# Half as many rows per DMA engine in an ifftshift of an 8192 x 8192 float32 matrix

## The chip, the core and the metric

The kernel runs on one core of one Trainium2 chip. The number that counts is the device time of one execution in microseconds; several runs are taken and their median is given. The profile is of one further execution with the hardware profiler on.

## The reference

```python
def setup_inputs():
    return {"x": np.random.randn(8192, 8192).astype(np.float32)}

def reference(x: np.ndarray) -> np.ndarray:
    return np.fft.ifftshift(x)
```

For even sizes an ifftshift over both axes swaps the four quadrants: `out[r, c] = x[(r + 4096) % 8192, (c + 4096) % 8192]`. Nothing is calculated. 268.4 MB are read from the device's memory and 268.4 MB are written to it.

## The kernel before

All the work is done by DMAs that go from the input tensor straight to the output tensor; no tile in on-chip memory is used and no compute engine has work. A row of the matrix has 8192 floats, 32 KB; a half row has `hc` = 4096 floats, 16 KB. `hr` = 4096 is half the number of rows.

The helper `both` (lines 25 to 34; the DMA itself has line 27 in the profile) issues one DMA on a queue. Its access pattern has three levels, `[[C, rows], [hc, 2], [1, piece]]` on the output: `rows` consecutive rows, in each row both halves, and in each half one contiguous run of `piece` floats that begins at column `col`. On the input side the same rows stand `hr` rows further on (modulo `R`), and the halves are taken in the opposite order (the step of the second level is `-hc`), so that each half lands in the other one.

The loops in lines 40 to 42 go over blocks of rows, and inside a block over the two values of `col`, 0 and `piece`. With `piece = hc // 2` (2048 floats, 8 KB) a DMA moves one quarter of both halves; the second DMA of a block moves the other quarter of the same rows. All DMAs are issued from SyncE (SP), on one queue, in the order of the loops.

A DMA is spread over the core's 16 DMA engines along its outermost level: with `rows = ENGINES * apart` (line 39) each engine gets `apart` neighbouring rows, so neighbouring engines work `apart` rows from each other. With `apart = 4` a DMA covers 64 rows, and each engine moves 4 rows x 2 halves = 8 packets of 8 KB. A further packet of 4 bytes on each engine then adds one to the DMA's semaphore; when all 16 have done so, the DMA has landed.

The framework gives the DMAs eight semaphores in turn (numbers 99 to 106 in the trace). SP issues the ninth DMA when the first has landed, the tenth when the second has, and so on: eight DMAs are in flight. These waits are not written in the kernel. Line 57 (start of the program) and line 68 (end of it) are what the profile gives for the launch code.

Of the kernel before, what the change touches and what calls it, by code (L numbers as in the profile page):

```python
# [1 line left out]

# [4 lines left out]


ENGINES = 16  # L10


@with_exitstack
def kernel(
    ctx: ExitStack,
    tc: tile.TileContext,
    x: bass.AP,
    out: bass.AP,
):
    nc = tc.nc  # L20
    R, C = x.shape
    hr = R // 2
    hc = C // 2

    def both(queue, row, col, rows, piece):

        queue.dma_start(
            out=bass.AP(out.tensor, out.offset + row * C + col, [[C, rows], [hc, 2], [1, piece]]),
            in_=bass.AP(
                x.tensor,  # L30
                x.offset + (row + hr) % R * C + hc + col,
                [[C, rows], [-hc, 2], [1, piece]],
            ),
        )


    apart = 4
    piece = hc // 2
    rows = ENGINES * apart
    for row in range(0, R, rows):  # L40
        for col in (0, piece):
            both(nc.sync, row, col, rows, piece)


# [1 line left out]
_INS = ['x']  # L46
_OUTS = [((8192, 8192), 'float32')]


def kernel(**inputs):  # L50
    import numpy as _np
    import concourse.bacc as _bacc
    import concourse.tile as _tile
    from concourse import mybir as _mybir
    from concourse.bass_utils import run_bass_kernel_spmd as _run

    nc = _bacc.Bacc("TRN2", target_bir_lowering=False, num_devices=1)  # L57
    arrays, args = {}, []
    for name in _INS:
        a = _np.ascontiguousarray(inputs[name])  # L60
        if a.dtype.kind in "iu":
            a = a.astype(_np.int64)
        arrays[f"in_{name}_dram"] = a
        args.append(nc.dram_tensor(f"in_{name}_dram", a.shape, _mybir.dt.from_np(a.dtype), kind="ExternalInput").ap())
    for i, (shape, dtype) in enumerate(_OUTS):
        dt = _mybir.dt.from_np(_np.dtype(dtype))
        args.append(nc.dram_tensor(f"out_{i}_dram", shape, dt, kind="ExternalOutput").ap())
    with _tile.TileContext(nc) as tc:
        kernel(tc, *args)
    r = _run(nc, [arrays], core_ids=[0])  # L70
    got = tuple(r.results[0][f"out_{i}_dram"] for i in range(len(_OUTS)))
    return got[0]
```

## Time and profile before

| | |
|---|---|
| median of 3 runs | 811.06 us (810.79 to 811.39) |
| the profiled execution | 810.44 us |
| its span, first to last instruction | 808.7 us |
| DMAs on SP's queue | 256 of 1024 KB, 25.1 us median from issue to landing |
| packets on that queue | 36864: 32768 of 8 KB and 4096 of 4 bytes |
| read / written in the device's memory | 268.44 MB / 268.44 MB, together 664 GB/s over the span |

How to read it: with no compute, the span is a chain of DMA traffic. The DMA row of the page gives, for 40 equal slices, the mean busy share of the 16 DMA engines in tenths (9 is 90% or more), and the GB/s row below it what they moved (bytes counted once, though each is read and written). Section 3 of the page gives the packets of each queue, and the share of 16 engines' span in which packets were running. An engine counts as busy while a packet of its own is under way, whether the packet moves at full speed or is held up. SP is shown by its waits.

### The profile page before, as it was taken

Reading aid. Unit: us, or ns where it says so; the run is one execution under the profiler, and the core shown is the slowest. Engines: PE = TensorE matmul, PEld = TensorE weight load, DVE = VectorE, ACT = ScalarE, POOL = GpSimd, SP = SyncE. Lnnn points to the kernel's source line nnn. Section 1 sums busy time; section 2 is a strip of 40 time slices with the busy share of each in tenths; the row PEclk is TensorE's granted clock in tenths of the full one; section 3 lists DMA queues with packets and bytes.
Section 4 is the critical chain, followed back from the end, with each engine's and each line's share of the span. In section 5 each row is a group of like instructions: output and inputs, shape, how many; then the busy total and the mean of one; then the engine's idle time right before and its main releaser. Section 6 shows DMA issues by size and latency. Waiting matters only on the chain. (4 is left out here: it accounts for less than half of the span.)

```text
span 808.7 us, 301 instructions
## 1 busy us (share of the span) xinstructions
POOL 0.2 (0%) x4
## 2 busy tenths in 40 slices
POOL 0000000000000000000000000000000000000000
DMA  8999999999999999999999999999999999999998
GB/s 301 331 335 329 336 334 330 335 332 336 332 335 334 336 331 334 339 328 335 331 335 339 334 334 337 331 336 330 336 334 331 339 332 334 333 336 331 337 335 294
DMA packets 36866, 268.47 MB, mean 332 GB/s; under 512 B 4096, under 2 KB 4096, under 8 KB 4096
## 3 DMA queue, kind: packets, MB, share of 16 engines
q1 hardware_dynamic: 36864, 268.45, 99.3%
q14 instruction: 2, 0.02, 0.0%
HBM read 268.44 MB, written 268.44 MB: 664 GB/s over the span
## 5 line engine op out<-in xcount | busy, mean ns | idle before, releaser
L57 POOL MEMSET const-bfloat16-1.0<- 128x1 bf16 x1 | 0.1, 102 | 0.0
L57 POOL MEMSET const-uint8-127<- 128x1 uint8 x1 | 0.1, 102 | 0.0
L57 POOL MEMSET const-float32-1.0<- 128x1 f32 x1 | 0.1, 99 | 0.0
L57 POOL MEMSET const-float32-0.0<- 128x1 f32 x1 | 0.1, 98 | 0.2 <-issue 0.2
## 6 DMA issues: line engine op xcount, KB each, us to landing
out_dram<-in_x_dram SPq DMA_DIRECT2D x256, 1024.0 KB, 25.1
```

The lines of the kernel that those rows point to most:

```text
L57: nc = _bacc.Bacc("TRN2", target_bir_lowering=False, num_devices=1)
```

## The change

```diff
--- before.py
+++ after.py
@@ -34,7 +34,7 @@
         )
 
 
-    apart = 4
+    apart = 2
     piece = hc // 2
     rows = ENGINES * apart
     for row in range(0, R, rows):
```

`rows` becomes 32. The loop over rows has 256 blocks in place of 128, and there are 512 DMAs of 0.5 MB in place of 256 of 1 MB. Each engine has 2 rows x 2 halves = 4 packets of 8 KB in a DMA, followed by its 4-byte packet. Neighbouring engines work 2 rows (64 KB) from each other in place of 4 rows (128 KB), the 16 engines of a DMA span 1 MB of each tensor in place of 2 MB, and an engine comes to the other quarter of its rows after 4 packets in place of 8. The 8 KB runs, the one queue, the eight semaphores and the bytes moved are the same.

## The prediction

> **What bounds the kernel now.** I read the page first, for who is busy at all:
>
> ```profile
> span 808.7 us, 301 instructions
> POOL 0.2 (0%) x4
> ...
> DMA  8999999999999999999999999999999999999998
> GB/s 301 331 335 329 336 334 330 335 332 336 332 335 334 336 331 334 339 328 335 331 335 339 334 334 337 331 336 330 336 334 331 339 332 334 333 336 331 337 335 294
> DMA packets 36866, 268.47 MB, mean 332 GB/s; under 512 B 4096, under 2 KB 4096, under 8 KB 4096
> ...
> q1 hardware_dynamic: 36864, 268.45, 99.3%
> ```
>
> No engine computes; the 16 DMA engines have a packet under way 99.3% of the span. The rate is flat: the inner slices lie between 328 and 339 GB/s. The 4096 packets under 512 B are the semaphore packets, 16 for each of 256 DMAs. Next, SP's own waits, to see if issuing holds the engines up:
>
> ```profile
> SPq L27 <- DMA out_dram<-in_x_dram: 634.0, 248, 3.2
> SPq L68 <- DMA out_dram<-in_x_dram: 24.1, 4, 15.2
> ```
>
> SP waits 634.0 us in 248 waits, 2.56 us each, for a landing before it may issue the next DMA: it is idle, not late. Then the view of stretches (columns: from:to, length, POOL busy, TensorE clock, DMA share, GB/s):
>
> ```profile
> 2.50:5.00 2.50, 0.00 (x0) 1.00 0.83 334
> 6.00:13.00 7.00, 0.00 (x0) 1.00 1.01 349
> 13.00:50.00 37.00, 0.00 (x0) 1.00 1.00 330
> 50.00:400.00 350.00, 0.00 (x0) 1.00 1.00 333
> 400.00:750.00 350.00, 0.00 (x0) 1.00 1.00 334
> ```
>
> Last, the single packet records of the trace. From 3.4 to 5.0 us nearly every 8 KB packet takes 309 ns, and the rate is 420 GB/s. From 6 to 13 us hardly any does: they take 380 ns on the mean, none under 309 and none over 526, at 349 GB/s. From 20 us on 62% take at most 316 ns and the rest are held up, to 1507 ns at worst; the mean is 391 ns, and 16 x 8192 B / 391 ns = 335 GB/s. So an engine alone could do its 2048 packets in 2048 x 309 ns = 633 us; it needs 2048 x 391 ns = 801 us, because 168 us of it are stalls. They come at nearly the same total rate whether all packets are slowed alike or a few are slowed much. I read that as a limit which the 16 engines share, on the memory's side (664 GB/s read and written), and not a limit of an engine or of SP.
>
> **The parts of the change.** The span splits into 2.2 us to the first packet, 805.4 us to the end of the last, and 1.1 us of ending. The profiled execution (810.44) is 0.6 us below the median; I add differences to the median, 811.06.
>
> *Twice the DMAs on SP.* 256 more issues of 562 ns (the records of line 27) are 144 us of SP's queue. A DMA of half the size takes 805.4 / 512 = 1.57 us of the engines, so SP issues for 0.56 us and still waits about 1.0 us each time: 0 on the path. If the cover were gone, 512 x 0.6 us = 307 us would still be below 805. At the start the first eight issues follow each other by 0.65 to 0.73 us, and a half DMA at the unhindered rate lasts 4 x 309 ns = 1.24 us: also covered.
>
> *Half the bytes in flight.* Eight DMAs are in flight as before. When one has landed, seven are left, 7 x 1.57 = 11.0 us of work in place of 22. The first and the last engine to finish a DMA are 1.9 us apart on the mean and 3.0 at most (landings on its semaphore), so the fastest engine still has about 8 us; from an issue to its first packet pass 1.45 us (0.73 to 2.18). Cost 0. The landing time should fall from 25.1 to about 8 x 1.57 = 12.6 us.
>
> *256 more semaphore packets on each engine.* Such a packet is recorded with 9 ns; the next data packet starts 3 ns after the end of the last one in place of 3 ns before it, so it costs 6 ns: 256 x 6 ns = 1.5 us. Ends: 0, where the stalls of the shared limit swallow it, and 256 x 9 ns = 2.3 us. I take 1.5, as 62% of the packets run at the engine's own pace. The packets behind a semaphore show no further cost. I followed each engine's packets from one semaphore to the next (2668 stretches that are unambiguous); the means by position in a DMA are 401, 388, 387, 400, 403, 384, 390 and 401 ns. Position 1, just behind a semaphore, is no dearer than 5, where there is none.
>
> The Trainium skill (DMA: Bandwidth & Descriptors, "Rules for kernel authors") asks for at least 1 MiB per DMA, and its fit gives a DMA a fixed 2.0 us. By that 256 more would cost up to 256 x 2.0 = 512 us if nothing hid it, and halving to 0.5 MB would be the wrong way. The share of 1.00 with eight DMAs in flight says that it is hidden here.
>
> *The addresses.* No row of the trace shows engines 64 KB apart. The positions above bound it: they fall in two classes, 401 ns (first half of an even row, second half of an odd one) and 387 ns (the other two), mean 394 for these stretches, so where a packet lies counts for +1.8% or -1.8%, though the mix stays 1:1 in the new order. If the new spacing pushed all packets into one class: +14 or -14 us. For no effect speaks that the spread between engines doubles over the run (1.1 us in the first eighths, 2.3 in the last) while the rate stays at 333 and 334. For a small loss speaks that the best inner slice is only 2% above the mean, but a held-up packet takes up to 1507 ns: a path that is this full has more to lose than to gain, and the 16 engines now crowd into 1 MB in place of 2. I take +2 us, near the zero that the flat rate shows.
>
> Sum: 811.06 + 0 + 0 + 1.5 + 2 = 814.5 us.
>
> On the spacing the same page ("Latency and other measured facts") has row pitches of 2 MiB and 4 MiB copying at 164 and 103 GB/s against 207 at 512 KiB. By it a smaller spacing doesn't lose, and the sum would be 812.6; no run here shows such pitches.
>
> **The rivals.** About 0.2% (1.6 us) is what a measurement of this kernel can tell from no change.
>
> 1. *The spacing is bad.* Closer engines meet in the same part of the memory more often, and packets go to the dear class: up to 811.06 + 14 + 1.5 = 827 us, middle 822. For: the class difference exists. Against: the flat rate.
> 2. *The spacing is good (the other side).* An engine returns to the other quarter of its rows after 4 packets, 1.6 us, in place of 3.1, and neighbours are closer; if parts of the memory that are still open are used again, packets go towards the cheap class: down to 811.06 - 14 + 1.5 = 799 us, middle 804. It decides when the mean packet falls below 390 ns by more than the semaphores cost. For: the 7 us at 349 GB/s show that the limit isn't a fixed number. Against: that rate was never held again.
> 3. *Hidden.* The shared limit swallows the semaphore packets and the addresses don't matter: 811 us. For: equal totals under all patterns of stalls. Against: address classes.
> 4. *A halt at each semaphore.* From a semaphore packet's end to its landing pass 0.58 us (mean). A DMA now takes 3.14 us against 8 x 309 ns + 6 ns = 2.48; if the missing 0.66 us were a halt for the semaphore, 256 more would cost 170 us: 981. Against: the stalls lie evenly over all eight positions.
>
> **How the numbers follow.** My forecast, slower by a little (812.7 to 820): 0.34. Rival 1, beyond 820: 0.19. Rival 4: 0.02. Rival 3, within 0.2%: 0.15. Rival 2, below 809.4: 0.30. So slower 0.55, same 0.15, faster 0.30. The range has to hold both signs: 799 (rival 2's end) to 828 (rival 1's end with 2.3 us for the semaphores); the likeliest case alone is 812.7 to 820.
>
> **What would show it.** 40960 packets on the queue, 8192 of them small; 512 issues of 512 KB landing in about 12.6 us; SP waiting about 1.0 us each; a share of 99% again. The address term is in the mean of the 8 KB packets: 392 ns for my sum, 387 or less for rival 2, 398 for rival 1. Longer packets just behind each semaphore would be rival 4. I'm wrong if SP's waits vanish, if the share falls below 98%, or if the mean packet moves by more than 1.8%.

## The result and the profile after

| | before | after |
|---|---|---|
| median of 11 runs each | 811.02 us (809.79 to 812.02) | 812.91 us (811.36 to 814.26) |
| ratio, 95% interval | | 1.0023 (1.0014 to 1.0033) |
| profiled execution / its span | 810.44 / 808.7 us | 814.26 / 812.5 us |

The changed kernel is slower by 1.9 us, with an interval of about 1.1 to 2.7 us. The ratios here and below are estimated from the runs as a whole and need not be the quotients of the medians to the last digit. The page of the changed kernel (slices, packets, queue, issues):

```profile
span 812.5 us, 557 instructions
...
DMA  8999999999999999999999999999999999999998
GB/s 298 330 337 331 334 328 333 334 333 335 331 327 332 337 332 333 330 334 328 335 333 336 332 330 332 336 330 334 329 331 335 334 332 332 334 333 330 336 336 282
DMA packets 40964, 268.50 MB, mean 330 GB/s; under 512 B 8192, under 2 KB 8192, under 8 KB 8192
...
q1 hardware_dynamic: 40960, 268.47, 99.1%
...
out_dram<-in_x_dram SPq DMA_DIRECT2D x512, 512.0 KB, 12.6
```

The change does what it says: 512 issues of half the size, 4096 more small packets, half the time to landing. The rate is as flat as before and the engines' share is the same within 0.2 points. SP's waits in the changed kernel (total us, times, longest):

```profile
SPq L27 <- DMA out_dram<-in_x_dram: 502.0, 502, 2.0
SPq L68 <- DMA out_dram<-in_x_dram: 11.8, 4, 7.4
```

502.0 / 502 = 1.0 us of waiting before each issue: SP is still idle more than it works. The view of stretches of the changed kernel (last columns: DMA share, GB/s):

```profile
6.00:13.00 7.00, 0.00 (x0) 1.00 0.97 355
13.00:50.00 37.00, 0.00 (x0) 1.00 1.00 332
50.00:400.00 350.00, 0.00 (x0) 1.00 1.00 332
400.00:750.00 350.00, 0.00 (x0) 1.00 1.00 333
```

In the long stretches it moves 332 and 333 GB/s where the kernel before had 333 and 334. The whole difference is of this size, one unit of the last digit, so a single profile can't settle it. The two profiled spans differ by 3.8 us, twice the difference of the medians, because this execution was the longest of the changed kernel's 11. When the changed kernel was run again (e9 below), its profiled span was 810.0 us. From here on ratios of many runs decide, each to the kernel before on the same chip, and the traces serve to exclude large effects.

The mean 8 KB packet is 391.0 ns in both traces. In e9, the same kernel once more, it is 389.5 ns, so a shift of 1 ns, which is 2 us of the kernel, can't be read from one trace. By position in a DMA it is 400, 386, 392 and 400 ns: the packet just behind a semaphore (400) is no dearer than the last one (400).

### The profile page after: what moved, and what is told of

Same layout as the page of the kernel before. It is cut to its first block, busy times and chain, and to the rows that moved or that the text cites. A ratio compares the mean times of both kernels' runs of the same rounds, so it can differ in the third digit from the quotient of the medians.

```text
span 812.5 us, 557 instructions
## 1 busy us (share of the span) xinstructions
POOL 0.2 (0%) x4
## 3 DMA queue, kind: packets, MB, share of 16 engines
q1 hardware_dynamic: 40960, 268.47, 99.1%
## 6 DMA issues: line engine op xcount, KB each, us to landing
out_dram<-in_x_dram SPq DMA_DIRECT2D x512, 512.0 KB, 12.6
```

## The experiments

Three theories stood against each other after the result. S: the semaphore packets alone, 6 ns each. A, later D: the distance between engines. F: fewer bytes in flight. After the first four runs a fourth came up, O: the order in which an engine goes through the quarters of its rows.

### e1: one row apart

The edit against the kernel before:

```diff
-    apart = 4
+    apart = 1
```

> 1 row apart, 1024 DMAs of 0.25 MB. Theory S (each further semaphore packet costs an engine 6 ns, nothing else counts): 768 more per engine than the kernel before, 768 x 6 ns = 4.6 us, 815.6 us; mean 8 KB packet 391 ns as in both kernels. Rival A (the spacing costs, about 1.9 us for each halving): 814.8 us, and the mean packet longer, 393 ns. Rival F (fewer bytes in flight let engines run dry): a DMA lasts 0.79 us of the engines, eight in flight are 6.3 us of work, so engines should go idle between packets: share under 98%, over 820 us.

Measured: 826.48 us, ratio 1.0196 (1.0183 to 1.0209). The page of e1:

```profile
span 825.3 us, 1069 instructions
...
DMA packets 49160, 268.57 MB, mean 325 GB/s; under 512 B 16384, under 2 KB 16384, under 8 KB 16384
...
q1 hardware_dynamic: 49152, 268.50, 99.4%
```

and its view of stretches:

```profile
50.00:400.00 350.00, 0.00 (x0) 1.00 1.00 327
400.00:750.00 350.00, 0.00 (x0) 1.00 1.00 327
```

F gave the right time for the wrong reason: the engines are not idle (99.4%, share 1.00), the packets are longer (396 ns on the mean). SP still waits in 472 of its issues:

```profile
SPq L27 <- DMA out_dram<-in_x_dram: 183.3, 472, 1.6
```

S and A, at 815, are both far too low. What makes the packets longer, the addresses or the many small DMAs, e1 alone doesn't tell; e2 does.

### e2: the same number of DMAs, engines 4 rows apart

The helper gets an outer step of `apart` rows, and a DMA takes one row of each four (the one-row level of the quoted pattern has `some` = 1). Each engine sees exactly the packets of the kernel before in the same order, with a semaphore after every second packet in place of every eighth. The lines shown are those of the output side and the loops; the input side gets the same outer step.

```diff
-                [[C, rows], [hc, 2], [1, piece]]
+                [[apart * C, ENGINES], [C, some], [hc, 2], [1, piece]]
...
         for col in (0, piece):
-            both(nc.sync, row, col, rows, piece)
+            for first in range(0, apart, some):
+                both(nc.sync, row + first, col, apart, some, piece)
```

> 1024 DMAs of 0.25 MB as in e1_one_row, but the engines stay 4 rows apart as in the kernel before: a DMA takes one row of each four. Theory S: 815.6 us, as e1_one_row. Rival A (spacing): 811.0 us, as the kernel before. Rival F: as e1_one_row, over 820 us with idle engines.

Measured: 811.92 us, ratio 1.0015 (1.0007 to 1.0024). The page and the stretches of e2:

```profile
span 809.9 us, 1069 instructions
...
DMA packets 49160, 268.57 MB, mean 332 GB/s; under 512 B 16384, under 2 KB 16384, under 8 KB 16384
...
q1 hardware_dynamic: 49152, 268.50, 99.6%
```

```profile
50.00:400.00 350.00, 0.00 (x0) 1.00 1.00 333
400.00:750.00 350.00, 0.00 (x0) 1.00 1.00 333
```

The packet line is that of e1, the rate is that of the kernel before. So neither 1024 DMAs nor 2 MB in flight make e1 slow (F falls); its addresses do, by distance or by order, and they cost 1.8% against e2. S falls too in its size: 768 more semaphore packets an engine take 768 x 6 ns = 4.6 us of each engine's time, but the kernel is only 1.2 us longer (0.6 to 1.9). Nearly three quarters are swallowed. The reading that fits is that engines which are held up by a limit they share lose little by 6 ns more. For the 256 of the change that makes about 0.4 us (0.2 to 0.6). This is an estimate, and a rough one, because e2 differs at its ends too. At the start SP issues a DMA of e2 every 0.63 us, and two packets take only 2 x 309 ns = 0.62 us: the packet records show each engine idle for 1.0 us up to 30 us, where the kernel before has 0.2 us. In the last 12 us it is the other way, 0.4 us against 1.3.

### e3 and e4: eight rows apart; one half in a DMA

Both edits are against the kernel before.

```diff
-    apart = 4
+    apart = 8
```

> 8 rows apart, 128 DMAs of 2 MB. Theory S: 128 semaphore packets less per engine, 128 x 6 ns = 0.8 us, 810.2 us. Rival A (spacing, 1.9 us for each doubling): 809.1 us, mean packet 390 ns. Rival F: as the kernel before, 811.0 us, since nothing runs dry there.

Measured: 812.59 us, ratio 1.0020 (1.0010 to 1.0030). All theories missed: with half the semaphores and twice the distance it is slower. It differs from the kernel before in two ways besides. An engine stays in a quarter for 16 packets. And SP's issues are held up: one takes 5.9 us (the median; up to 14.4) where the kernel before has 0.56, and no wait for a landing stands before them. The page of e3 gives the time from issue to landing:

```profile
out_dram<-in_x_dram SPq DMA_DIRECT2D x128, 2048.0 KB, 42.0
```

A DMA takes the engines 811.3 / 128 = 6.3 us, so 42.0 us to landing mean 6 to 7 DMAs in flight in place of eight, about 13 MB. This trace doesn't show what holds the issues up; the engines' share is 99.7% even so.

The edit of e4:

```diff
-            both(nc.sync, row, col, rows, piece)
+            for half in (0, 1):
+                one(nc.sync, row, half, col, rows, piece)
```

Here `one` has the pattern `[[C, rows], [1, piece]]` on both sides, with the halves swapped in the offsets.

> 4 rows apart, 512 DMAs of 0.5 MB: a DMA takes one quarter of one half of 64 rows, 4 packets an engine. DMA count and size of the changed kernel, spacing of the kernel before; the two halves of a row are no longer neighbours in an engine's order. Theory S: 812.5 us. Rival A (spacing): 811.0 us. Rival F (bytes in flight): 812.9 us as the changed kernel. If the order of the halves matters, the mean 8 KB packet moves away from 391 ns and the time with it, 2.05 us for each ns.

Measured: 813.25 us, ratio 1.0034 (1.0022 to 1.0045). The mean packet of its trace is 390.5 ns, near the 391 as it was. The distance is that of the kernel before, and still 0.3% are lost, more than the 0.05% of the semaphores. The order of an engine's packets counts, then. (In e4 it is the order of the halves that differs.) That led to O: in the changed kernel an engine turns to the other quarter of its rows after 4 packets in place of 8.

### e5 to e8: order and distance taken apart

e5 and e6 have the DMAs of e2 (4 rows apart) in another order; e7 and e8 are 2 rows and 1 row apart, but turn to the other quarter only after 8 packets.

```diff
 e5, against e2
-        for col in (0, piece):
-            for first in range(0, apart, some):
+        for pair in range(0, apart, 2):
+            for col in (0, piece):
+                for first in (pair, pair + 1):
 e6, against e2
-        for col in (0, piece):
-            for first in range(0, apart, some):
+        for first in range(0, apart, some):
+            for col in (0, piece):
 e7 (apart = 2) and e8 (apart = 1), against the kernel before
-    for row in range(0, R, rows):
-        for col in (0, piece):
-            both(nc.sync, row, col, rows, piece)
+    for block in range(0, R, ENGINES * 4):
+        for col in (0, piece):
+            for row in range(block, block + ENGINES * 4, rows):
+                both(nc.sync, row, col, rows, piece)
```

> Engines 4 rows apart, 1024 DMAs of 0.25 MB as e2_far_tiny, but an engine goes through its rows in the order of the changed kernel: two rows in one quarter, the same two rows in the other quarter, then the next two. Reference: e2_far_tiny, 811.9 us, which differs in this order alone. Theory D (the distance between engines is what costs): 811.9 us. Rival O (the order costs: turning to the other quarter after 4 packets in place of 8): 811.9 + 1.5 = 813.4 us.

> Engines 4 rows apart, 1024 DMAs of 0.25 MB, but an engine goes through its rows in the order of e1_one_row: one row in one quarter, the same row in the other, then the next row. Theory D (distance): 811.9 us as e2_far_tiny, mean 8 KB packet 389 ns. Rival O (order): 826 us as e1_one_row, mean packet 396 ns.

> Engines 2 rows apart, 512 DMAs of 0.5 MB as the changed kernel, but two neighbouring blocks of 32 rows are done in one quarter before both are done in the other: an engine turns to the other quarter after 8 packets, as in the kernel before. Theory D (distance): 812.9 us as the changed kernel. Rival O (order): 811.0 + 0.4 for the semaphores = 811.4 us.

> Engines 1 row apart, 1024 DMAs of 0.25 MB as e1_one_row, but four blocks of 16 rows are done in one quarter before all four are done in the other: an engine turns to the other quarter after 8 packets. Theory D (distance): 826 us as e1_one_row, mean 8 KB packet 396 ns. Rival O (order): 811.9 us as e2_far_tiny, mean packet 389 ns.

These four ran on a chip on which the kernel before takes 821.69 us (819.82 to 823.06, 17 runs), so only ratios are compared.

| | rows apart | turns after | DMAs | median us | ratio (95%) |
|---|---|---|---|---|---|
| e5 | 4 | 4 packets | 1024 | 825.25 | 1.0043 (1.0029 to 1.0057) |
| e6 | 4 | 2 packets | 1024 | 825.01 | 1.0037 (1.0023 to 1.0050) |
| e7 | 2 | 8 packets | 512 | 822.19 | 1.0004 (0.9995 to 1.0012) |
| e8 | 1 | 8 packets | 1024 | 837.11 | 1.0153 (1.0110 to 1.0197) |

e7 speaks for O: the distance of the changed kernel, its DMA size and count, and nothing is lost beyond the semaphores. e5 and e6 agree with O in sign against e2's 1.0015 from another chip. But e6, which turns after 2 packets, is no dearer than e5, and far from the ratio 1.0196 of e1 that O gave it (826 us was meant for the other chips). e8 speaks for D at one row: the late turn doesn't bring it back. The size is rough, as one of its six runs took 827 us and the others 835 to 840; the quotient of its medians would be 1.0188. Its stretches:

```profile
50.00:400.00 350.00, 0.00 (x0) 1.00 1.00 321
400.00:750.00 350.00, 0.00 (x0) 1.00 1.00 326
```

against e7 on the same chip:

```profile
50.00:400.00 350.00, 0.00 (x0) 1.00 1.00 329
400.00:750.00 350.00, 0.00 (x0) 1.00 1.00 329
```

The mean packet is 400.3 ns in e8 and 394.9 ns in e7. So both theories hold, each in its range: the order costs a little at 2 and 4 rows, the distance costs much at 1 row. Distance here is more than one thing: in e1 and e8 an engine's own next row lies 16 rows on, not beside the last one, and no run takes the two apart.

The pair e7 and e8 also bears out how a DMA's rows are dealt to the engines. If an engine got every sixteenth row in place of neighbouring ones, e7 would send each engine the same packets in the same order as e8, and only the semaphores would differ; but the two are 1.5% apart, and 768 more semaphores in e2 made 0.15%.

### e9 to e12: the deciding ones on one chip

e9 is the changed kernel, e10 is e7 and e11 is e2 once more. e12 is the kernel before with a later turn:

```diff
-    for row in range(0, R, rows):
-        for col in (0, piece):
-            both(nc.sync, row, col, rows, piece)
+    for block in range(0, R, 2 * rows):
+        for col in (0, piece):
+            for row in range(block, block + 2 * rows, rows):
+                both(nc.sync, row, col, rows, piece)
```

> The changed kernel once more, to stand on one chip beside the next three. All ratios are to the kernel before on the same chip. Theory O (the order costs: turning to the other quarter after 4 packets): ratio 1.002. Theory D (distance between engines): also 1.002; this run is their common reference.

> e7_two_rows_late on this chip: engines 2 rows apart, 512 DMAs, turning after 8 packets. Theory O: ratio 1.0005 (the semaphores alone), clearly below e9_changed_again. Theory D: 1.002, as e9_changed_again.

> e2_far_tiny on this chip: packet order and distances of the kernel before, four times its semaphore packets. If the semaphores are mostly swallowed by the shared limit: ratio 1.0015, mean 8 KB packet about 1.5 ns shorter than in the kernel before on this chip. If each costs its 6 ns: 1.0057.

> Engines 4 rows apart, 256 DMAs of 1 MB as the kernel before, but two blocks of 64 rows are done in one quarter before both are done in the other: an engine turns after 16 packets. Theory O, if a later turn goes on helping: 0.999 or less. If 8 packets are enough, or by theory D: 1.000.

The kernel before: 810.72 us (809.76 to 812.42, 35 runs).

| | rows apart | turns after | DMAs | median us | ratio (95%) |
|---|---|---|---|---|---|
| e9 | 2 | 4 packets | 512 | 812.47 | 1.0024 (1.0015 to 1.0032) |
| e10 | 2 | 8 packets | 512 | 811.17 | 1.0004 (0.9995 to 1.0013) |
| e11 | 4 | 8 packets | 1024 | 812.10 | 1.0015 (1.0006 to 1.0023) |
| e12 | 4 | 16 packets | 256 | 811.77 | 1.0010 (1.0001 to 1.0018) |

All three repeated ratios came out again within 0.0001. e9 and e10 issue the very same 512 DMAs, in another order, and their intervals don't overlap: the order is worth 1.3 us by the medians (1.6 by the ratios). e12 is not below 1: turning later than after 8 packets doesn't help. Its interval even lies just above 1, and e3, which also turns after 16 packets, was at 1.0020. Their mean packets, 393.1 and 394.5 ns, are longer than the 391.0 of the kernel before. So O is not the simple rule that later is better; of the orders tried, the turn after 8 packets is the best. e11's ratio fits semaphores that are mostly swallowed. Its mean packet, 390.2 ns, is 0.8 ns below the 391.0 of the kernel before and not 1.5; with 391.0 and 389.5 for two traces of the changed kernel, that decides nothing. None of the 12 beats the kernel before.

The pages and stretches of e9 and e10 show why single profiles could hardly have told it. Of e9:

```profile
span 810.0 us, 557 instructions
...
q1 hardware_dynamic: 40960, 268.47, 99.1%
```

```profile
50.00:400.00 350.00, 0.00 (x0) 1.00 1.00 333
400.00:750.00 350.00, 0.00 (x0) 1.00 1.00 333
```

and of e10:

```profile
span 809.4 us, 557 instructions
...
q1 hardware_dynamic: 40960, 268.47, 99.1%
```

```profile
50.00:400.00 350.00, 0.00 (x0) 1.00 1.00 334
400.00:750.00 350.00, 0.00 (x0) 1.00 1.00 334
```

Same packets, same share, spans nearer to each other (0.6 us) than their medians (1.3 us), mean packets of 389.5 and 389.3 ns, and rates that differ by one unit of the last digit.

Why the order costs is not settled. The first and the last engine finish a DMA 2.9 us apart on the mean in e9 and 3.0 us in e10, so the traces show no different spread of the engines. No run here looks inside the memory.

## Why the prediction came out as it did

Forecast: 814.5 us, slower by 3.4. Measured: 812.91, slower by 1.9. The sign and the case (slower by a little) were right; both terms of the sum were too large, and the second stood on a wrong reason. So the sign was partly luck, and so was the case: its range began at 812.7, 0.2 us below what was measured. Two readings in the working are slightly off and change nothing: the sum adds up to 814.6, and the first issues follow each other by 0.63 to 0.73 us.

- **A limit that the engines share, not SP and not an engine of its own.** Right as to SP and the engines: four times the DMAs at unchanged addresses (e2, e11) cost 0.15%. That the limit lies on the memory's side fits e1, which differs from e2 in addresses alone and is 1.8% slower, but no run shows where it lies.
- **Twice the DMAs on SP: 0.** Right: 1.0 us of waiting per issue was forecast and measured.
- **Half the bytes in flight: 0.** Right: 12.6 us to landing as forecast, 99.1% share, and e2 with a quarter of the bytes in flight keeps 99.6%.
- **256 semaphore packets on each engine: 1.5 us.** Right mechanism, mis-sized: about 0.4 us, estimated as a third of e2's excess. In the changed kernel's trace the next data packet starts 5 or 6 ns after the semaphore's start, as before, so the 6 ns are spent. The step that failed was "as 62% of the packets run at the engine's own pace" to count them in full. The lower end, that the shared limit swallows them, was the nearer one.
- **The addresses: 2 us, for engines that crowd into 1 MB.** The size was near, the reason wrong, and the agreement luck. e10 has the same crowding and is at 1.0004. What costs is the order in which the same DMAs come: e9 against e10, 1.3 us. In e9 an engine comes back to the other quarter of its rows after 4 packets; e5 agrees in sign, across chips, and e4 shows another order that costs. Why they cost stays open, and so does whether any part of the memory is "still open". The prediction named this early return, but in rival 2 and as a gain. The mark that it gave for this term, a mean packet of 392 ns, can't be told apart from no change: 391.0 and 389.5 ns were measured in two traces of one kernel. Both lie away from rival 1's 398 and above rival 2's 387. That closer engines cost is true one step further: at one row e8 loses 1.5%, of which e2 puts 0.15% down to the semaphores. So the prediction's sentence that by the row pitches a smaller spacing doesn't lose agrees with 64 KB and fails at 32 KB.
- **A halt at each semaphore (981 us).** Excluded: e2 has 1024 of them on each engine and takes 811.92 us.
- **The 2.0 us for each DMA.** The Trainium skill (DMA: Bandwidth & Descriptors, "Rules for kernel authors") asks for at least 1 MiB per DMA for the full bandwidth. With eight in flight, DMAs of 0.25 MB still move 333 GB/s in e2. The Trainium skill gives its fit of a fixed 2.0 us (the same page, "Anatomy of one DMA — SWDGE (gpsimd) path") for DMAs that GpSimd issues, and here SyncE issues them. The 768 more DMAs of e2 cost 1.2 us all together.

By the terms: 0.4 (semaphores, an estimate) + 1.3 (order) + 0 (distance) = 1.7 of the 1.9 us measured, well inside the interval. The 0 for the distance is as good as e10's interval, which holds -0.4 to +1.1 us for distance and semaphores together.

## What to carry to other kernels

When a profile shows all DMA engines busy and yet many packets held up, as here, look for a bound that they share. Overhead added to the single engines was mostly swallowed in this case (1.2 of 4.6 us came through), so price it from zero upwards, not in full. Changing a tiling constant moves several things at once (size, count, distance, order); write the loop so that each can be changed alone before one of them is blamed. For effects of 0.2% compare medians of many runs on one chip; two profiled spans can differ by twice the effect.

## What the runs showed of the hardware

- Engines 1 row (32 KB) apart lose 1.5 to 2.0% (e8, e1), while 64 KB and 128 KB can't be told apart (e10 at 1.0004). The step from 2 rows to 1 is sudden, and it is in the length of the packets (396 ns in e1 against 389 ns in e2), not in idle engines.
- The order of the same packets within a few microseconds is worth 0.2 to 0.3% (e9 against e10, and e4); of the orders tried none beat the turn after 8 packets (e12 and e3, after 16: 1.0010 and 1.0020).
- With DMAs of 2 MB SP's issues themselves take 5.9 us in place of 0.56 and 6 to 7 are in flight (e3).
- Chips can differ by more than the change: the kernel before took 810.7 to 811.0 us in three of the four comparisons and 821.7 us in the other, on another chip, 1.3% longer, with the same ratio between the kernels where it was tried on two (e7 and e10, both 1.0004).
